# Decay series split between the first products and POOL, first norm inside the fourth x tile, gate banks assigned by hand, and another order at attention's end

## The chip, the cores and the metric

One core of a Trainium2 chip runs the whole program. Its engines work side by side, each through its own list of instructions in order: TensorE does the matmuls (PE in the profile, PEld for its weight loads), VectorE (DVE), ScalarE (ACT) and GpSimd (POOL) do elementwise work, SyncE (SP) and POOL issue DMA transfers. Matmul results lie in eight PSUM banks of 128 x 512 float32. The metric is the device time in microseconds.

## The reference

Two layers on x of shape (1, 512, 1024). Each is a token mixer and then a SwiGLU feed-forward part, with an RMS norm ahead of each part and plain residual adds; a final norm follows. Layer 0 mixes with a gated linear recurrence, layer 1 with stick-breaking attention (16 heads of 64). What bears on the change is the recurrence:

```python
proj = h @ w_in                                  # h = rmsnorm(x)
gate_br, x_br = proj[..., :D_RNN], proj[..., D_RNN:]
gate = gelu(gate_br)
xc = causal_depthwise_conv(x_br, conv_w, conv_b) # width 4
r = sigmoid(blockdiag(xc, w_r) + b_r)            # 4 blocks of 256
i = sigmoid(blockdiag(xc, w_i) + b_i)
log_a = 8.0 * r * log_sigmoid(lam)
a = exp(log_a)
u = sqrt(max(-expm1(2 * log_a), 0)) * (i * xc)
hs = linear_scan(a, u)                           # h_t = a_t h_(t-1) + u_t
return (hs * gate) @ w_out
```

`log_sigmoid(lam)` is a function of 1024 constants; the kernel works it out as a series on a tile of 128 x 8 ("decay").

## The kernel before

**Matmuls.** Every float32 operand is split in a rounded part and a residue (`wh` and `wl` for weights, `uh` and `ul` for activations), and `mm3` makes each product from three matmuls (lines L348 to L350). `mm_tile` does one output tile of 128 x 512 from 8 k-steps of three matmuls. Weights come in chunks of 128 x 1024: SP loads chunk i into one of 4 `raw` buffers, ACT casts it to `wh` (L312), and DVE or POOL subtracts to get `wl` (L313), into 3 buffers each. `wl_on` says which engine does it for chunks 2 to 21; we write wl(i) for this step of chunk i.

**The recurrence (`rglru`).** PE's order is: x tiles 0 and 1 together (`tile_x2`, k by k as x arrives), x tiles 2 to 6, gates(0), x tile 7, gates(1), gate tiles 0 and 1, gates(2), gate tile 2, gates(3), gate tiles 3 to 7, then the output product. x tile m uses chunk m up to 6; chunk 7 belongs to gates(0), chunk 8 to x tile 7. gates(n) has four groups of six matmuls, one bank each.

The norm is applied after the product: `norm_sq` sums the squares of x into `acc` (squares on ACT, adds on DVE, L462), `norm_rs1` forms the row sums with tiny matmuls (L480) and the reciprocal roots on ACT and DVE (`rsqrt`, L467 to L474, which ends with four diagonal blocks `dg`), and `norm_rs2` spreads them over a bank with matmuls (L488) and copies that to `acc` (`rsB`, L489, ACT). `norm_rs1` stands at the middle of x tile 3, `norm_rs2` at the middle of x tile 4.

`evac_x(m)` takes x tile m from its bank once `rsB` is there: times `rsB` (L580, DVE), the convolution (L581 on ACT, three L583 on DVE), and the split into `ah` (L585, ACT) and `al` (L586, DVE), which gates(m // 2) reads. For m of 2 and more the convolution reads the bank itself, so that the bank is free only after the last L583; tiles 0 and 1 are first copied out by L580. evac_x runs for tiles 0 to 2 after x tile 4, then for three more after each further x tile.

`decay` (L561 to L572) is 18 operations on DVE on tiles of 128 x 8, put behind the diagonals by `issue_after`; its results are the scales `ncl`, which gates(0) reads first (L610, tanh on ACT), and `cl`, read by the chain of exponentials (L615). `chain` then does the scan for four tiles (L618 to L624 on DVE). A gate tile leaves its bank by L694 (DVE).

**Banks.** `ps()` hands out the 8 banks in rotation (`bi % 8`). The 2 first x tiles take 0 and 1, tile 2 takes 2, tile 3 takes 3, `norm_rs1` 4, tile 4 5, `norm_rs2` 6, tile 5 7, tile 6 0; gates(0) then takes 1, 2, 3, 4, tile 7 takes 5, gates(1) 6, 7, 0, 1, gate tile 0 takes 2 and gate tile 1 takes 3, gates(2) 4 to 7, gate tile 2 0, gates(3) 1 to 4.

**What sets the order.** In `tile_x2`, in attention's second part and in the feed-forward part the order of the engines' instructions is as written (`manual_schedule`). In the rest of `rglru` a scheduler orders each engine's list by priority (program order; the splits of weights ahead of it) and by when it expects inputs.

**Attention's end.** Heads run in a pipeline: iteration h issues s1(h + 1), chain_a(h + 1), s3(h - 1), s2(h), chain_b(h) and the evacuation `s3_evac(h - 1)` (L1269 on ACT, L1270 on DVE). From h = 13 on one of the two banks for s3 is taken by the output product, so that s3(h) has to wait for s3_evac(h - 1). In iterations 13 and 14 `out_split` also splits a chunk of output weights, with the cast on DVE; in 14 its residue is on DVE too, in 13 on POOL.

Of the kernel before, what the change touches and what calls it, by code (L numbers as in the profile page):

```python
# [10 lines left out]
F32 = mybir.dt.float32  # L11
# [15 lines left out]
RG_C = 8.0  # L27
# [143 lines left out]
class Kern:  # L171
    def __init__(self, ctx, tc, a, out):
        self.ctx, self.tc, self.nc, self.a, self.out = ctx, tc, tc.nc, a, out
        mk = lambda name, bufs, **kw: ctx.enter_context(tc.tile_pool(name=name, bufs=bufs, **kw))
        self.const = mk("const", 1)
        self.wp = mk("wp", 1)
        self.tp = mk("tp", 1)
        self.ar = mk("ar", 1)
        self.free = deque((0, i) for i in range(NS1))
        self.free2 = deque()  # L180
        self.clock = 0
        self.keep2 = 0
        self.slot = {}
        pp = mk("pp", 1, space=bass.MemoryType.PSUM)
        self.bank = [pp.tile([P, S], F32, name=f"bank{i}") for i in range(8)]
        self.bi = 0
        self.tn = 0
        self.later, self.done, self.chain = [], set(), {}
        self.wl_dve = self.wh_dve = False
        self.ring4 = None  # L190
        self.wl_on = {**dict.fromkeys((*range(5, 12), 14, 18, 20, 21), self.nc.gpsimd),
                      **dict.fromkeys((2, 3, 4, 12, 13, 15, 16, 17, 19), self.nc.vector)}

    def ps(self):
        b = self.bank[self.bi % 8]
        self.bi += 1
        return b

# [104 lines left out]
    def split_one(self):  # L303
        i = self.split
        with self.tc.high_priority(self.PRI):
            e = self.chunks[i]
            if isinstance(e, Piece):
                e.sums()
            raw = e.source() if isinstance(e, Piece) else self.raw.pop(i)
            wh, wl = self.split_tiles(i)  # L310
            c = slice(0, raw.shape[-1])
            (self.nc.vector.tensor_copy if self.wh_dve else self.nc.scalar.copy)(wh[:, c], raw)  # L312
            self.wl_engine(i).tensor_tensor(wl[:, c], raw, wh[:, c].bitcast(F32), ALU.subtract)  # L313
            if isinstance(e, Piece):
                e.after()

# [35 lines left out]
    def mm_tile(self, out, xs, mid=None):  # L352
        wh, wl = self.chunk()
        n = len(xs)
        for k in range(n):
            if mid and k == n // 2:
                mid()
            xh, xl = xs[k]
            self.mm3(out, wh[:, ts(k)], wl[:, ts(k)], xh, xl, k == 0, k == n - 1)

# [188 lines left out]
    def rglru(self):  # L549
        nc, tc = self.nc, self.tc  # L550
        with ExitStack() as cx:
# [6 lines left out]
            tc.keep_in_program_order(nc.scalar.preload_act_table_set("natural_log_exp_and_others"))  # L558
            ncl = w

            def decay():  # L561
                nc.vector.tensor_scalar(z, w, 2.0, None, ALU.add)
                nc.vector.reciprocal(z, z)
                nc.vector.tensor_tensor(z, z, w, ALU.mult)
                nc.vector.tensor_tensor(z2, z, z, ALU.mult)
                nc.vector.tensor_scalar(pl, z2, 2.0 / 21, None, ALU.mult)
                for n in (19, 17, 15, 13, 11, 9, 7, 5, 3):
                    nc.vector.scalar_tensor_tensor(pl, pl, 2.0 / n, z2, ALU.add, ALU.mult)
                nc.vector.scalar_tensor_tensor(pl, pl, 2.0, z, ALU.add, ALU.mult)
                nc.vector.scalar_tensor_tensor(cl, lam, 0.0, pl, ALU.min, ALU.subtract)  # L570
                nc.vector.tensor_scalar(cl, cl, RG_C, None, ALU.mult)
                nc.vector.tensor_scalar(ncl, cl, -1.0, 0.0, ALU.mult, ALU.max)  # L572

            def evac_x(m, ps):
                xc[m], ah[m], al[m] = self.new("xc"), self.new("ah", F32R, True), self.new("al", F32R, True)
# [14 lines left out]
            def tile_x(m, mid=None):  # L590
                p = self.ps()
                self.mm_tile(p, self.u, mid)
                return p
# [45 lines left out]
            def tile_x2():  # L639
                p = (self.ps(), self.ps())  # L640
                hl = [self.split_tiles(i) for i in range(2)]
                for k in range(KT):
                    self.norm_in(k, "g_mix0", False)
                    wh, wl = hl[k // 4]
                    if k in self.first:
                        src = self.first[k]
                        c = slice(k % 4 * 2 * P, k % 4 * 2 * P + src.shape[-1])
                        nc.scalar.copy(wh[:, c], src)  # L648
                        nc.vector.tensor_tensor(wl[:, c], src, wh[:, c].bitcast(F32), ALU.subtract)
                    if k == 3:  # L650
                        nc.scalar.activation(w, lam, AF.Abs)
                        nc.scalar.activation(w, w, AF.Exp, scale=-1.0)
                    for i in range(2):
                        c = ts(2 * (k % 4) + i)
                        self.mm3(p[i], wh[:, c], wl[:, c], *self.u[k], k == 0, k == KT - 1)
                nc.gpsimd.memset(self.ones, 1.0)
                nc.gpsimd.memset(self.ident, 0.0)
                nc.gpsimd.affine_select(out=self.ident, in_=self.ident, compare_op=ALU.not_equal, fill=1.0,
                                        base=0, pattern=[[-1, P]], channel_multiplier=1)
                for i in range(2):  # L660
                    self.wq.pop(i)
                self.used = 2
                return p

            pend = []
            for m in range(KT):
                if m == 0:
                    with tc.manual_schedule(engines={mybir.EngineType.Activation, mybir.EngineType.DVE}):
                        pend = list(enumerate(tile_x2()))
                    continue  # L670
                if m == 1:
                    continue
                pend.append((m, tile_x(m, {3: self.norm_rs1, 4: self.norm_rs2}.get(m))))
                if m == 2:
                    with tc.issue_after(self.uhi.ins):
                        for k in range(KT):
                            self.norm_sq(k, nc.vector)
                        nc.scalar.activation(self.st[:, 0:1], self.ones[:, 0:1], AF.Sqrt)
                if m == 3:
                    with tc.issue_after(self.dgi.ins):  # L680
                        decay()
                if m >= 4:
                    for q in pend[:3]:
                        evac_x(*q)
                    pend = pend[3:]
                if m in (6, 7):
                    gates(m - 6)
# [377 lines left out]
    def attention(self):  # L1065
# [5 lines left out]
        with ExitStack() as cx:  # L1071
# [201 lines left out]
            with tc.manual_schedule(engines={E.PE, E.Activation, E.DVE, E.Pool}):  # L1273
# [45 lines left out]
                for h in range(NH + 1):  # L1319
# [40 lines left out]
                        chain_b(h)  # L1360
                    if h == 15:
                        s3(h - 1)
                    if h in (13, 14):
                        out_split()
                    if h >= 1:
                        s3_evac(h - 1)
                    if t < 16 and t % 2 == 0:
                        proj_evac2(t)
                    if 6 <= h < 14 and 2 * nsp + 1 < h:
# [102 lines left out]
```

## Time and profile before

| | |
|---|---|
| median of 3 runs | 1105.23 us (1105.14 to 1107.29) |
| profiled execution | 1105.78 us, span 1104.1 us |
| PE busy | 1088.8 us (99%) |
| DVE, ACT, POOL busy | 901.5 (82%), 709.5 (64%), 363.4 us (33%) |
| mean granted TensorE clock | 0.998 |

The span runs from the first to the last instruction of the program; the profiled execution's own time is 1.7 us longer. Busy times are shares of that span. Matmuls are pipelined, so a busy PE need not be at its peak, and its rows overlap: the distance between two starts tells more than a row's duration.

### The profile page before, as it was taken

The numbers are of one execution on the slowest core, as the hardware profiler recorded it, in microseconds if no ns is written. First come the engines' busy times: TensorE is split into PE (matmuls) and PEld (weight loads), VectorE is DVE, ScalarE is ACT, GpSimd is POOL, SyncE is SP. The second block draws the span as 40 slices with busy tenths as digits, with TensorE's granted clock in tenths as the row PEclk, the third lists the DMA queues.
The fourth block names the chain that finished last, engine by engine and source line by source line (L and its number), as shares of the span: only waits on it lengthen the run. The fifth ranks groups of instructions, "written<-read, shape, count | busy, mean of one in ns | idle before, by whom it ended". The sixth has DMA issues, their size and how long they took to land.

```text
span 1104.1 us, 14724 instructions
## 1 busy us (share of the span) xinstructions
PE 1088.8 (99%) x5255; PEld 907.8 (82%) x5255; DVE 901.5 (82%) x1261; ACT 709.5 (64%) x1084; POOL 363.4 (33%) x251
## 2 busy tenths in 40 slices
PE   9999999999999999999999999999999999999996
PEld 6788888888888888988888888788888888888885
DVE  6978887696978888986378898978679897978897
ACT  6498567565646464635379999967765555546454
POOL 1444242325151514205034445413132424151412
PEclk9999999999999999999999999999999999999999
DMA  8513338887776776343243433225987777775532
GB/s 303 154 59 98 118 111 209 199 191 191 157 200 156 204 155 185 82 152 96 69 122 96 121 90 96 62 94 135 214 175 207 164 186 173 157 199 119 148 69 76
DMA packets 47385, 159.87 MB, mean 145 GB/s; under 512 B 5712, under 2 KB 5968, under 8 KB 47312
## 3 DMA queue, kind: packets, MB, share of 16 engines
q1 hardware_dynamic: 34640, 113.32, 32.0%
q0 software_dynamic: 12384, 45.09, 23.7%
q8 instruction: 41, 0.67, 0.2%
q10 hardware_dynamic: 288, 0.52, 0.1%
q14 instruction: 32, 0.26, 0.1%
HBM read 148.43 MB, written 2.10 MB: 136 GB/s over the span
## 4 chain that ended last, share of the span: by engine, by line
PE 75%; DVE 9%; ACT 4%; issue 3%; DVEq 0%
PE bank L763 17%; PE bank L764 17%; PE bank L765 17%; PE bank L348 6%; PE bank L350 6%; PE bank L349 6%; DVE wl L313 3%; PE bank L1230 2%; DVE y L755 1%; PE bank L770 1%; PE bank L1256 1%; ACT t L1194 1%; ACT t L1193 1%; ACT wh L312 1%; DVE ks L1159 1%
## 5 line engine op out<-in xcount | busy, mean ns | idle before, releaser
L312 ACT CAST wh<-raw 128x1024 fp32r<-128x1024 f32 x134 | 140.2, 1048 | 95.4 <-PE bank L765 36.0
L313 DVE TENSOR_TENSOR wl<-raw,wh 128x1024 fp32r<-128x1024 f32 x112 | 168.3, 1506 | 36.5 <-ACT wh L312 36.4
L763 PE MATMUL bank<-wh,ow 128*128 128x512 f32 (+1 forms) x480 | 179.7, 374 | 0.5 <-DVE b L755 0.5
L765 PE MATMUL bank<-wh,ow 128*128 128x512 f32 (+1 forms) x480 | 178.4, 372 | 0.0
L764 PE MATMUL bank<-wl,ow 128*128 128x512 f32 (+1 forms) x480 | 178.3, 371 | 0.0
L92 POOL DMA_DIRECT2D bu<-w_gu x64 | 56.5, 883 | 275.4 <-DMA bu<-w_gu 147.5
L312 ACT CAST wh<-bu 128x1024 fp32r<-128x1024 f32 x66 | 69.4, 1053 | 65.4 <-PE bank L765 36.1
L313 DVE TENSOR_TENSOR wl<-bu,wh 128x1024 fp32r<-128x1024 f32 x66 | 82.7, 1270 | 30.2 <-ACT wh L312 29.3
L763 PEld LDWEIGHTS bank<-wh,ow 128*128 128x128 f32 x480 | 90.4, 188 | 17.1 <-issue 1.6
L765 PEld LDWEIGHTS bank<-wh,ow 128*128 128x128 f32 x480 | 90.4, 188 | 15.8
L764 PEld LDWEIGHTS bank<-wl,ow 128*128 128x128 f32 x480 | 90.4, 188 | 15.3
L348 PE MATMUL bank<-uh,wh 128*128 128x512 f32 x256 | 102.2, 401 | 0.3 <-ACT wh L648 0.3
L349 PE MATMUL bank<-ul,wh 128*128 128x512 f32 x256 | 99.8, 391 | 0.0
L350 PE MATMUL bank<-uh,wl 128*128 128x512 f32 x256 | 99.6, 391 | 0.0
L755 DVE TENSOR_TENSOR y<-y,bank 128x512 f32<-128x512 f32 x140 | 88.9, 678 | 2.2 <-PE bank L765 2.1
L313 POOL TENSOR_TENSOR wl<-raw,wh 128x1024 fp32r<-128x1024 f32 x24 | 61.1, 2547 | 88.6 <-ACT wh L312 77.5
L763 PE MATMUL bank<-wh,hth 128*128 128x512 f32 (+1 forms) x194 | 75.4, 389 | 0.0
L764 PE MATMUL bank<-wl,hth 128*128 128x512 f32 (+1 forms) x194 | 75.2, 388 | 0.0
L765 PE MATMUL bank<-wh,htl 128*128 128x512 f32 (+1 forms) x194 | 75.1, 387 | 0.0
L313 DVE TENSOR_TENSOR wl<-bv,wh 128x1024 fp32r<-128x1024 f32 x44 | 58.3, 1336 | 13.2 <-ACT wh L312 13.2
L1198 POOL TENSOR_TENSOR spl<-t,sph 128x512 fp32r<-128x512 f32 (+1 forms) x32 | 39.1, 1242 | 82.6 <-DVE sph L1197 80.7
L312 ACT CAST wh<-bv 128x1024 fp32r<-128x1024 f32 x44 | 45.8, 1049 | 18.0 <-PE bank L765 9.0
(276 smaller groups left out, 2776.2 us busy)
## 6 DMA issues: line engine op xcount, KB each, us to landing
bu<-w_gu POOLq DMA_DIRECT2D x64, 512.0 KB, 5.8
raw<-w_gu SPq DMA_DIRECT2D x44, 512.0 KB, 4.0
raw<-w_dn SPq DMA_DIRECT2D x24, 512.0 KB, 5.8
bu<-w_gu SPq DMA_DIRECT2D x22, 512.0 KB, 4.3
bv<-w_gu SPq DMA_DIRECT2D x22, 512.0 KB, 4.2
bv<-w_gu POOLq DMA_DIRECT2D x22, 512.0 KB, 6.4
d<-w_dn SPq DMA_DIRECT2D x20, 512.0 KB, 3.6
raw<-w_qk SPq DMA_DIRECT2D x16, 512.0 KB, 3.6
```

What stands on the lines that cost most here:

```text
L92: kern.soon(lambda: kern.nc.gpsimd.dma_start(t, self.part(n), accum_op=ALU.add))
L312: (self.nc.vector.tensor_copy if self.wh_dve else self.nc.scalar.copy)(wh[:, c], raw)
L313: self.wl_engine(i).tensor_tensor(wl[:, c], raw, wh[:, c].bitcast(F32), ALU.subtract)
L348: mm(out, lhsT=wh, rhs=xh, start=first, stop=False)
L349: mm(out, lhsT=wh, rhs=xl, start=False, stop=False)
L350: mm(out, lhsT=wl, rhs=xh, start=False, stop=last)
L755: add = lambda o, a, b: nc.vector.tensor_tensor(o, a, b, ALU.add)
L763: mm(out, lhsT=xh, rhs=wh, start=first, stop=False, skip_group_check=True)
L764: mm(out, lhsT=xh, rhs=wl, start=False, stop=False, skip_group_check=True)
L765: mm(out, lhsT=xl, rhs=wh, start=False, stop=last, skip_group_check=True)
L1198: nc.gpsimd.tensor_tensor(sl[:, w], sp[:, w], sh[:, w].bitcast(F32), ALU.subtract)
L1230: mm(zt[kt][:, o0:o0 + ZW[j]], lhsT=tri if j == kt else one_n, rhs=s_, start=False, stop=True, skip_group_check=True)
```

## The change

- The decay series is cut in two. Its first five operations (`decay1`) stay on DVE and move ahead of the third k-step of `tile_x2`; their input (Abs and Exp on ACT) moves from the fourth k-step to the second. The other 13 become 24 operations on POOL (`decay2`, a fused DVE operation being two on POOL), issued after wl(7) of x tile 6.
- `norm_rs1` moves from the middle of x tile 3 to after its first k-step, `norm_rs2` from the middle of x tile 4 to after the fifth k-step of x tile 3.
- wl(5) and wl(6) move from POOL to DVE, wl(5) behind the diagonals.
- `ps()` follows a list by hand for its calls 9 to 19: gates(0) gets banks 4, 5, 1, 2, x tile 7 gets 3, gates(1) gets 6, 7, 4, 5, gate tiles 0 and 1 get 1 and 2. By the moved norm x tile 4 lies in bank 6 and `norm_rs2` in 5. gates(3) keeps 1 to 4.
- At attention's end `s3_evac(h - 1)` comes before `out_split`.

```diff
+        self.swap = dict(zip(range(9, 20), (4, 5, 1, 2, 3, 6, 7, 4, 5, 1, 2)))
...
-        self.wl_on = {**dict.fromkeys((*range(5, 12), 14, 18, 20, 21), self.nc.gpsimd),
-                      **dict.fromkeys((2, 3, 4, 12, 13, 15, 16, 17, 19), self.nc.vector)}
+        self.wl_on = {**dict.fromkeys((*range(7, 12), 14, 18, 20, 21), self.nc.gpsimd),
+                      **dict.fromkeys((2, 3, 4, 5, 6, 12, 13, 15, 16, 17, 19), self.nc.vector)}
...
-        b = self.bank[self.bi % 8]
+        b = self.bank[self.swap.pop(self.bi, self.bi % 8)]
...
-            self.wl_engine(i).tensor_tensor(wl[:, c], raw, wh[:, c].bitcast(F32), ALU.subtract)
+            with self.tc.issue_after(self.dgi.ins) if i == 5 else ExitStack():
+                self.wli = self.wl_engine(i).tensor_tensor(wl[:, c], raw, wh[:, c].bitcast(F32), ALU.subtract)
...
-            if mid and k == n // 2:
-                mid()
+            if mid and k in mid:
+                mid[k]()
...
-            def decay():
+            def decay1():
                 nc.vector.tensor_scalar(z, w, 2.0, None, ALU.add)
                 nc.vector.reciprocal(z, z)
                 nc.vector.tensor_tensor(z, z, w, ALU.mult)
                 nc.vector.tensor_tensor(z2, z, z, ALU.mult)
                 nc.vector.tensor_scalar(pl, z2, 2.0 / 21, None, ALU.mult)
-                for n in (19, 17, 15, 13, 11, 9, 7, 5, 3):
-                    nc.vector.scalar_tensor_tensor(pl, pl, 2.0 / n, z2, ALU.add, ALU.mult)
-                nc.vector.scalar_tensor_tensor(pl, pl, 2.0, z, ALU.add, ALU.mult)
-                nc.vector.scalar_tensor_tensor(cl, lam, 0.0, pl, ALU.min, ALU.subtract)
-                nc.vector.tensor_scalar(cl, cl, RG_C, None, ALU.mult)
-                nc.vector.tensor_scalar(ncl, cl, -1.0, 0.0, ALU.mult, ALU.max)
+
+            def decay2():
+                e = nc.gpsimd
+                for c, y in *((2.0 / n, z2) for n in (19, 17, 15, 13, 11, 9, 7, 5, 3)), (2.0, z):
+                    e.tensor_scalar(pl, pl, c, None, ALU.add)
+                    e.tensor_tensor(pl, pl, y, ALU.mult)
+                e.tensor_scalar(cl, lam, 0.0, None, ALU.min)
+                e.tensor_tensor(cl, cl, pl, ALU.subtract)
+                e.tensor_scalar(cl, cl, RG_C, None, ALU.mult)
+                e.tensor_scalar(ncl, cl, -1.0, 0.0, ALU.mult, ALU.max)
...
                 for k in range(KT):
+                    if k == 2:
+                        decay1()
...
-                    if k == 3:
+                    if k == 1:
                         nc.scalar.activation(w, lam, AF.Abs)
                         nc.scalar.activation(w, w, AF.Exp, scale=-1.0)
...
-                pend.append((m, tile_x(m, {3: self.norm_rs1, 4: self.norm_rs2}.get(m))))
+                pend.append((m, tile_x(m, {1: self.norm_rs1, 5: self.norm_rs2} if m == 3 else None)))
...
-                if m == 3:
-                    with tc.issue_after(self.dgi.ins):
-                        decay()
+                if m == 6:
+                    with tc.issue_after(self.wli.ins):
+                        decay2()
...
+                    if h >= 1:
+                        s3_evac(h - 1)
                     if h in (13, 14):
                         out_split()
-                    if h >= 1:
-                        s3_evac(h - 1)
```

## The prediction

> **What bounds the kernel now.** I read the page first, then the list of waits of the matmul engine (PE), then timelines around its longest waits.
>
> ```profile
> span 1104.1 us, 14724 instructions
> ...
> PE 1088.8 (99%) x5255; PEld 907.8 (82%) x5255; DVE 901.5 (82%) x1261; ACT 709.5 (64%) x1084; POOL 363.4 (33%) x251
> ```
>
> PE is busy for 1088.8 of 1104.1 us. The change leaves the matmuls as they are, so all that it can win is idle time of PE, 15.3 us in all, and of that only the waits that it touches. What it does to DVE (82%) or POOL (33%) counts only where PE comes to wait for it. The list of PE's waits (who waits, for whom, us in total, times, longest) has three candidates:
>
> ```profile
> PE bank L348 <- DVE xc L583: 2.1, 1, 2.1
> PE bank L385 <- DVE warm L383: 1.3, 1, 1.3
> PE bank L1256 <- DVE o L1270: 0.9, 2, 0.7
> ...
> PE bank L348 <- DVE gt L694: 0.4, 1, 0.4
> ```
>
> The second is the start. The others stand in PE's timeline as pairs of neighbours (start, duration, idle before):
>
> ```profile
> 48.90 0.39 PE L349 MATMUL bank<-al,wh 128*128 128x512 f32 x1
> 49.13 0.39 PE L350 MATMUL bank<-ah,wl 128*128 128x512 f32 x1
> 51.58 0.47 PE L348 MATMUL bank<-ah,wh 128*128 128x512 f32 x1 [2.06 <-DVE xc L583]
> ...
> 89.85 0.39 PE L350 MATMUL bank<-ah,wl 128*128 128x512 f32 x1
> 90.68 0.50 PE L348 MATMUL bank<-ah,wh 128*128 128x512 f32 x1 [0.44 <-DVE gt L694]
> ...
> 714.14 0.67 PE L1256 MATMUL bank<-awh,vs 128*128 128x512 f32 x2 [0.67 <-DVE o L1270]
> ```
>
> Neighbours normally start 0.23 us apart (48.90 to 49.13). So the first wait costs 2.45 - 0.23 = 2.2 us, the second 0.83 - 0.23 = 0.6, the third its idle time, 0.67.
>
> **Part 1: norm and decay leave DVE's path, and gates(0) gets other banks.** The wait at 51.58 is in the third of the four groups of gates(0). By the rotation this group writes bank 3, which holds x tile 3 until evac_x(3) on DVE is through (its last L583). Why DVE is late, in the timelines of POOL and of DVE:
>
> ```profile
> 26.28 2.71 POOL L313 TENSOR_TENSOR wl<-raw,wh 128x1024 fp32r<-128x1024 f32 x1
> ...
> 30.52 2.38 POOL L313 TENSOR_TENSOR wl<-raw,wh 128x1024 fp32r<-128x1024 f32 x1 [0.68 <-ACT wh L312]
> 39.12 2.85 POOL L313 TENSOR_TENSOR wl<-raw,wh 128x1024 fp32r<-128x1024 f32 x1 [6.22 <-ACT wh L312]
> 45.58 2.40 POOL L313 TENSOR_TENSOR wl<-raw,wh 128x1024 fp32r<-128x1024 f32 x1 [3.61 <-ACT wh L312]
> ```
>
> ```profile
> 20.36 3.87 DVE L462 TENSOR_TENSOR acc<-acc,t 128x512 f32<-128x512 f32 x5
> 27.29 1.74 DVE L470 SCALAR_TENSOR_TENSOR x<-x 128x4 f32<-128x4 f32 x1
> 29.45 0.87 DVE L474 TENSOR_SCALAR t<-x,x 128x128 f32<-128x128 f32 x4
> 30.24 0.17 DVE L562 TENSOR_SCALAR sm<-sm 128x8 f32<-128x8 f32 x1
> 30.68 2.24 DVE L564 TENSOR_TENSOR sm<-sm 128x8 f32<-128x8 f32 x1
> 33.36 1.77 DVE L568 SCALAR_TENSOR_TENSOR sm<-sm 128x8 f32<-128x8 f32 x9
> 35.85 1.28 DVE L580 TENSOR_TENSOR xb<-bank,acc 128x512 f32<-128x512 f32 x2
> ```
>
> (Rows: start, duration, engine, line, operation, tiles, shapes, count, idle before.) The decay series holds DVE from 30.24 to 35.85, 5.6 us; only then does the first evacuation (L580) start. Two tiny operations took ten times the 0.17 of their neighbour: 1.74 and 2.24. Both times POOL was inside a residue operation `wl`, the rows at 26.28 and 30.52. They end at 28.99 and 32.90, DVE's two at 29.03 and 32.92. These two are wl(5) and wl(6), the ones that move to DVE, so both blocks vanish. The Trainium skill says the same ("SBUF — State Buffer", section "Who interferes with whom"): DVE and GpSimd hold a shared port pair exclusively, and a DVE instruction with two SBUF inputs is shut out while a GpSimd instruction reads SBUF. These rows agree, and its other half, that GpSimd waits likewise behind DVE, is a rival below.
>
> When the norm can start:
>
> ```profile
> 23.69 0.39 PE L348 MATMUL bank<-uh,wh 128*128 128x512 f32 x1
> 25.73 0.39 PE L480 MATMUL bank<-x,acc 128*128 128x1 f32 x3
> ...
> 26.54 0.49 PE L348 MATMUL bank<-uh,wh 128*128 128x512 f32 x1
> ...
> 32.13 1.05 PE L488 MATMUL bank<-t,x 128*128 128x128 f32 x8
> ```
>
> Tile 3 starts three matmuls before 23.69, at 23.01. The row sums (L480) come at 25.73, after 12 of its matmuls, and the broadcast (L488) 12 matmuls into tile 4, both exactly where the program puts them, so I take the new places as kept too. Then L480 is due at 23.69, after k = 0, but the sum of squares ends at 20.36 + 3.87 = 24.23 (DVE has nothing less to do before it). PE waits until about 24.3: **a new wait of 0.6 us**. Bounds: 0, if the scheduler lets later matmuls pass, and 0.7 with a semaphore's time on top; I take 0.6, since order was kept before.
>
> ```profile
> 33.22 0.59 ACT L489 COPY acc<-bank 128x512 f32<-128x512 f32 x1 [2.79 <-PE bank L488]
> ```
>
> ```profile
> 16.68 1.23 DVE L313 TENSOR_TENSOR wl<-raw,wh 128x1024 fp32r<-128x1024 f32 x1 [0.25 <-ACT wh L312]
> ```
>
> The chain behind it: from L480's first start to the end of the diagonals (29.45 + 0.87 = 30.32) took 4.6 us; without the block of 1.74 - 0.17 = 1.6 it is 3.0. So they are ready at 27.3. PE meanwhile has eight L480 (0.8 us: 25.73 to 26.54, where tile 3 goes on) and 12 matmuls (2.7 us), and asks for them at 27.8: no wait, 0.5 us of slack. The broadcast and the copy to `acc` on ACT took from 32.13 to 33.81; from 27.8 they end at 29.5. DVE has wl(5) in between, covered by that wait: 1.23 us by DVE's own row of this shape, from 27.3 to 28.5.
>
> So evac_x starts near 29.6 instead of 35.85, 6.2 us sooner; wl(6) takes 1.2 of it back, 5.0 remain. The new banks ask for less besides: gates(0) gets 4, 5 (the norm's, long free), 1 (tile 1, already copied out) and 2 (tile 2). Tile 7 gets bank 3, two groups of six matmuls after the place where the old wait fell. Late by 2.2 before, early by 5: **2.2 us are won**, and the 0.6 above goes off.
>
> decay1 (five tiny DVE operations, at 1.77 / 9 = 0.2 us each, 1.0 us) stands ahead of the third k-step. There DVE idles:
>
> ```profile
> 8.63 0.75 DVE L407 SCALAR_TENSOR_TENSOR ul<-x,x,uh 128x512 fp32r<-128x512 f32 x1 [1.25 <-ACT uh L406]
> ```
>
> ```profile
> 7.87 0.72 ACT L406 ACTIVATE uh<-x,x 128x512 fp32r<-128x512 f32 x1 [1.41 <-DMA x<-xp]
> ```
>
> ```profile
> 7.59 0.54 POOL L1093 TENSOR_SCALAR_AFFINE_SELECT x<-x 128x128 bf16<-128x128 bf16 x2
> ```
>
> 1.25 us hold 1.0; Abs and Exp go into ACT's own hole of 1.41, in which it waits for the DMA of the same x tile. Cost 0; at most 0.3 if POOL's pair of operations at 7.59 (0.54) blocks one of the five (1.0 + 0.54 - 1.25).
>
> decay2 has 24 tiny operations on POOL behind wl(7), the row at 39.12 that ends at 41.97. Nearest row, the reader of decay2's result, and the first matmul of tile 7:
>
> ```profile
> L1198 POOL TENSOR_TENSOR spl<-sp,sph 128x384 fp32r<-128x384 f32 x16 | 19.5, 1219 | 9.1 <-DVE sph L1197 6.9 <-PE bank L1230 2.1
> ```
>
> ```profile
> 54.39 0.39 PE L348 MATMUL bank<-uh,wh 128*128 128x512 f32 x1
> 57.41 0.73 ACT L610 ACTIVATE sv<-r,sm 128x512 f32<-128x512 f32 x1
> ```
>
> Shapes of 384 and 1024 columns take 1.22 (with blocks in it) and 2.40 (45.58): 1.8 ns a column, so 0.5 us for none. The bounds for one are the 0.2 of DVE's tiny ones (33.36) and 1.2; I take 0.3, nearer to the tiny shape. Then decay2 ends at 41.97 + 7.2 = 49.2, and wl(8), queued behind it (2.40), at 51.6. It is needed 0.45 us into tile 7, which now starts at 54.39 - 2.2 + 0.6 = 52.8, so by 53.2. The first reader of the result (L610, 57.41 before) is later still. Cost 0. It turns into a cost at (53.2 - 2.4 - 41.97) / 24 = 0.37 us an operation.
>
> **Part 2: gates(3).** Its wait at 90.68 is for bank 3, its third group, whose holder (gate tile 1) DVE evacuates late:
>
> ```profile
> 63.59 0.78 ACT L581 ACTIVATE xc<-bank,x 128x512 f32<-128x512 f32 x1 [1.71 <-DVE bank L580]
> ...
> 89.97 0.66 DVE L694 TENSOR_TENSOR gt<-bank,acc 128x512 f32<-128x512 f32 x1
> ```
>
> By the new list gate tile 1 lies in bank 2, the second group, so PE asks for it six matmuls (1.4 us) sooner: alone, that makes the wait 0.6 + 1.4 = 2.0. But ACT stood idle for 1.71 us before 63.59, since DVE came to tile 7 late; with DVE 5 us ahead that goes, and everything that ACT and DVE queue behind it up to L694 moves up by at least 1.7 us more than PE does. Taken: the wait vanishes, **0.6 us won**; bounds, 0.6 won and 1.4 lost.
>
> **Part 3: s3_evac before out_split.** At h = 13 DVE has the cast of weights first:
>
> ```profile
> 712.81 0.68 DVE L312 CAST wh<-raw 128x1024 fp32r<-128x1024 f32 x1
> 713.41 0.67 DVE L1270 TENSOR_TENSOR o<-bank,t 64x512 f32<-64x512 f32 x1
> ```
>
> L1270 then starts at 712.81, 0.6 us sooner, and PE's wait of 0.67 shrinks by that: **0.6 us won**. The cast goes back by 0.6, and with it its wl on POOL and the spl (L1198) queued there; PE is asked for nothing of these before s2(15), and the weights are read one iteration on. At h = 14 no PE wait is tied to L1270. Cost 0, at most 0.2.
>
> **Sum:** -2.2 + 0.6 - 0.6 - 0.6 = -2.8 us. The profiled execution took 1105.78 us (its span and 1.7 around it), which gives 1103.0. The median of the three runs, 1105.23, lies 0.55 below that execution, so I predict 1102.5 us. A measurement of this kernel tells about 0.2%, 2.2 us, from no change.
>
> **Rivals.** (A) The banks of gates(3) turn against it, 2.0 instead of 0.6: -2.2 + 0.6 + 1.4 - 0.6 = -0.8, median near 1104.4. For it: L694 stands behind the scans in DVE's order, and the scheduler may keep it there. Against it: ACT's hole of 1.71.
>
> (B) The norm's waits take the place of the old one: PE waits 0.6 for the sums and, if the chain keeps its 4.6 us, another 1.1 at the broadcast (24.3 + 4.6 = 28.9 against 27.8). Sum -2.2 + 1.7 - 0.6 - 0.6 = -1.7, median 1103.5: the change moves the wait and wins too little to be told. For it: 0.5 us of slack only. Against it: POOL has no residue to work on then.
>
> (C) Slower: decay2 crawls on POOL. If every operation first waits out a DVE operation of 0.7 us, one takes about 0.8: 19.2 us, wl(8) ends at 41.97 + 19.2 + 2.4 = 63.6, 10.4 after it is needed; the time is +7.6, near 1113. It loses all gains from 0.49 us an operation on ((53.2 + 2.8 - 2.4 - 41.97) / 24). Against it: most of what DVE does then (L580, L583) reads a bank and one SBUF tile, and wl(7) and wl(8) at 39.12 and 45.58 took 2.85 and 2.40 beside it, hardly blocked. The exclusive lock of the page named above is what would make it so. A further rule of the skill speaks for it: by "GPSIMD Engine Reference", section "2.1 Instruction dispatch", the first call to a freshly loaded kernel on POOL pays about 6 us. No row here shows such a gap; with it decay2 would end near 55, 4.4 us be lost at tile 7, and the sum be +1.6 (an estimate from that page).
>
> **How the numbers follow.** Forecast 0.57, A 0.15, B 0.16, C 0.12. Inside the forecast the size runs from -2.2 (one of the small gains missing) to -3.4 (no wait for the sums), 1101.8 to 1103.1, and the median of few runs adds some 0.5 on each side: its own range is 1101.3 to 1103.6. With A and B, to 1105; C's far end is left out. Faster by over 0.2%: the forecast without its weak edge and a little of B, 0.53; slower: most of C, 0.11; the same: the rest, 0.36.
>
> **What would show it.** L580 starts near 30 instead of 35.85, and PE's waits for L583 and L694 are gone: Part 1 and 2 right. A wait of PE's L480 for `acc` of about 0.5 shows the price. L1270 ahead of L312 near 711, and L1256's longest wait under 0.2: Part 3. Wrong, if PE waits for wl L313 of POOL near 53, or L488 for the diagonals, or L348 for L694 with 1 us or more.

## The result, and the profile after

The changed kernel takes 1102.93 us (median of 8 runs, 1102.49 to 1104.74) beside 1106.72 us for the kernel before (8 runs, 1105.14 to 1108.16): a ratio of 0.9969, 95% interval 0.9958 to 0.9979, some 3.4 us by the ratio (3.8 between the medians). The profiled execution took 1102.71 us; its span fell from 1104.1 to 1101.0. First the head of the page of the changed kernel, then its list of what PE waits for (us in total, times, longest):

```profile
span 1101.0 us, 14735 instructions
...
PE 1087.4 (99%) x5255; PEld 907.8 (82%) x5255; DVE 896.4 (81%) x1250; ACT 710.8 (65%) x1084; POOL 363.5 (33%) x273
```

```profile
PE bank L350 <- ACT wh L656: 1.4, 2, 1.2
PE bank L387 <- DVE warm L385: 1.3, 1, 1.3
...
PE bank L350 <- DVE gt L702: 0.4, 1, 0.4
PE bank L1264 <- DVE o L1278: 0.2, 1, 0.2
```

The wait of 2.1 for x tile 3 is gone from the list. So is the one of 0.67 in attention; the 0.2 for `o` that is left stood beside it before (0.9 in two waits). The one of gates(3) for the gate tile (0.4) is still there. Nothing new stands in the list but a longer wait at the start. Where the time came from shows when the same matmuls are lined up (start, duration): the first of gates(0), the first of tile 7, one ahead of attention, one early in attention, the one in attention whose wait is gone, one near the end. After:

```profile
46.92 0.39 PE L350 MATMUL bank<-ah,wh 128*128 128x512 f32 x1
...
52.36 0.39 PE L350 MATMUL bank<-uh,wh 128*128 128x512 f32 x1
...
466.40 0.39 PE L773 MATMUL bank<-wh,htl 128*128 128x512 f32 x1
...
699.28 0.40 PE L352 MATMUL bank<-oh,wl 128*128 128x512 f32 x1
...
711.39 0.80 PE L1264 MATMUL bank<-awh,vs 128*128 128x512 f32 x3
...
1068.37 0.39 PE L773 MATMUL bank<-wh,htl 128*128 128x512 f32 x1
```

Before (the first of tile 7 stood at 54.39, the one in attention at 714.14):

```profile
46.63 0.39 PE L348 MATMUL bank<-ah,wh 128*128 128x512 f32 x1
...
468.88 0.39 PE L765 MATMUL bank<-wh,htl 128*128 128x512 f32 x1
...
701.77 0.40 PE L350 MATMUL bank<-oh,wl 128*128 128x512 f32 x1
...
1071.46 0.39 PE L765 MATMUL bank<-wh,htl 128*128 128x512 f32 x1
```

The changed kernel is 0.3 late at 46.92, 2.0 ahead at tile 7, 2.5 ahead at 466.40 and still at 699.28, 2.75 ahead at 711.39, and 3.1 ahead at 1068.37. So gates(0) gave 2.3, the stretch from 53 to 466 some 0.4, attention 0.25, the stretch behind it some 0.35 in small pieces, and the start took 0.3. In attention the wait at 711.39 did shrink by 0.6, but PE lost 0.35 just ahead of it, from 709.6 to 710.5, where the lead falls from 2.50 to 2.15. The start is the DMA of an x tile: ACT waited for it until 8.22 here and until 7.87 before.

```profile
8.22 0.72 ACT L408 ACTIVATE uh<-x,x 128x512 fp32r<-128x512 f32 x1 [1.55 <-DMA x<-xp]
```

How the norm runs now, on PE and on DVE:

```profile
23.28 0.39 PE L350 MATMUL bank<-uh,wh 128*128 128x512 f32 x1
...
24.87 0.95 PE L482 MATMUL bank<-x,acc 128*128 128x1 f32 x8
...
27.63 1.05 PE L490 MATMUL bank<-t,x 128*128 128x128 f32 x8
```

```profile
23.87 0.69 DVE L464 TENSOR_TENSOR acc<-acc,t 128x512 f32<-128x512 f32 x1
...
26.43 0.16 DVE L472 SCALAR_TENSOR_TENSOR x<-x 128x4 f32<-128x4 f32 x1
...
29.34 1.29 DVE L586 TENSOR_TENSOR xb<-bank,acc 128x512 f32<-128x512 f32 x2 [0.30 <-ACT acc L491]
```

Tile 3 starts at 23.28, but the row sums (L482) come at 24.87, after seven of its matmuls and not after three. The last sum of squares ends at 23.87 + 0.69 = 24.56, so PE waits for nothing. The tiny operation that took 1.74 before takes 0.16, and the first evacuation (L586) starts at 29.34 instead of 35.85.

The series on POOL: its first operation, a plain one, its last, and the residues behind it:

```profile
39.99 0.57 POOL L573 TENSOR_SCALAR sm<-sm 128x8 f32<-128x8 f32 x1
...
40.85 0.20 POOL L574 TENSOR_TENSOR sm<-sm 128x8 f32<-128x8 f32 x1
...
48.15 0.26 POOL L578 TENSOR_SCALAR sm<-sm 128x8 f32<-128x8 f32 x1
48.37 5.22 POOL L315 TENSOR_TENSOR wl<-raw,wh 128x1024 fp32r<-128x1024 f32 x2
```

24 operations in 48.41 - 39.99 = 8.4 us: 0.35 each on average, of which the typical 0.20 to 0.24 is work and the rest the step to the next; three of them took 0.57, 0.69 and 0.67. wl(8) begins at 48.37.

The wait that stayed, at gates(3): on PE, then DVE's chain that leads to it, after and (second fence, its first row alone) before:

```profile
86.14 0.39 PE L352 MATMUL bank<-ah,wl 128*128 128x512 f32 x1
86.93 0.50 PE L350 MATMUL bank<-ah,wh 128*128 128x512 f32 x1 [0.41 <-DVE gt L702]
...
68.97 1.30 DVE L624 SCALAR_TENSOR_TENSOR sv<-t,sv 128x512 f32<-128x512 f32 x2 [2.53 <-ACT t L623]
...
86.22 0.66 DVE L702 TENSOR_TENSOR gt<-bank,acc 128x512 f32<-128x512 f32 x1
```

```profile
72.72 1.30 DVE L618 SCALAR_TENSOR_TENSOR sv<-t,sv 128x512 f32<-128x512 f32 x2 [2.53 <-ACT t L617]
```

From the chain's first row to the gate tile's evacuation it is 17.25 us in both (68.97 to 86.22, 72.72 to 89.97): a rigid block, moved up by 3.75 as a whole. And the attention's two operations, in their new order:

```profile
710.66 0.67 DVE L1278 TENSOR_TENSOR o<-bank,t 64x512 f32<-64x512 f32 x1
711.26 0.67 DVE L313 CAST wh<-raw 128x1024 fp32r<-128x1024 f32 x1
```

### The profile page after: what moved, and what is told of

Its sections match the earlier page's. It is cut to its first block, busy times and chain, and to the rows that moved or that the text cites. A ratio compares the mean times of both kernels' runs of the same rounds, so it can differ in the third digit from the quotient of the medians.

```text
span 1101.0 us, 14735 instructions
## 1 busy us (share of the span) xinstructions
PE 1087.4 (99%) x5255; PEld 907.8 (82%) x5255; DVE 896.4 (81%) x1250; ACT 710.8 (65%) x1084; POOL 363.5 (33%) x273
## 4 chain that ended last, share of the span: by engine, by line
PE 75%; DVE 9%; ACT 4%; issue 3%; DVEq 0%
PE bank L771 17%; PE bank L772 17%; PE bank L773 17%; PE bank L350 6%; PE bank L352 6%; PE bank L351 6%; DVE wl L315 3%; PE bank L1238 2%; DVE y L763 1%; PE bank L778 1%; PE bank L1264 1%; ACT t L1202 1%; ACT t L1201 1%; ACT wh L313 1%; DVE ks L1167 1%
## 5 line engine op out<-in xcount | busy, mean ns | idle before, releaser
L315 DVE TENSOR_TENSOR wl<-raw,wh 128x1024 fp32r<-128x1024 f32 x114 | 171.6, 1507 | 39.9 <-ACT wh L313 39.5
L315 POOL TENSOR_TENSOR wl<-raw,wh 128x1024 fp32r<-128x1024 f32 x22 | 55.8, 2540 | 80.1 <-ACT wh L313 68.4
L350 PEld LDWEIGHTS bank<-uh,wh 128*128 128x128 f32 x256 | 48.0, 188 | 11.5 <-ACT wh L656 2.5
```

The costliest lines, as they stand in the source:

```text
L315: self.wli = self.wl_engine(i).tensor_tensor(wl[:, c], raw, wh[:, c].bitcast(F32), ALU.subtract)
L350: mm(out, lhsT=wh, rhs=xh, start=first, stop=False)
```

## The experiments

The theory (D in the expectations): the gain is VectorE's time. PE pays where VectorE is late, and any part counts only by how much sooner VectorE gets on. The rivals put the gain elsewhere: in the banks by hand (K), in the series leaving VectorE, in the port that VectorE shares with POOL; or they see a price in POOL's load (C of the prediction). All comparisons are with the kernel before, on the same chip.

**1. The banks, each way.** The changed kernel with the plain rotation:

```diff
-        self.swap = dict(zip(range(9, 20), (4, 5, 1, 2, 3, 6, 7, 4, 5, 1, 2)))
+        self.swap = {}
```

> The changed kernel with the plain rotation of banks in place of the list by hand: gates(0) gets 1, 2, 3, 4, x tile 7 gets 5, gates(1) 6, 7, 0, 1, gate tiles 0 and 1 get 2 and 3. Theory D (DVE starts the evacuations 6.5 us sooner, and this alone ends PE's wait in gates(0)): tile 3 leaves bank 3 by about 46, the third group asks for it at 49.7, so no wait comes back; gate tile 1 is asked for in the third group of gates(3) again, 1.4 us later than now, so the 0.6 us left there go too: span about 1100.4. Theory K (the banks by hand end the wait, DVE's earlier start is not needed): the wait for L589 comes back in the third group of gates(0), up to 2.2 us: span about 1103.

And the kernel before with such a list and nothing else:

```diff
+        self.swap = dict(zip(range(9, 20), (4, 6, 1, 2, 3, 5, 7, 4, 6, 1, 2)))
...
-        b = self.bank[self.bi % 8]
+        b = self.bank[self.swap.pop(self.bi, self.bi % 8)]
```

> The kernel before with banks by hand alone, fitted to its own place of the norm: gates(0) gets 4, 6, 1, 2, x tile 7 gets 3, gates(1) 5, 7, 4, 6, gate tiles 0 and 1 get 1 and 2. Decay, norm and splits stay as they were. Theory K: PE's wait of 2.1 us goes and nothing comes for it; gates(3) asks 1.4 us sooner for gate tile 1: span 1104.1 - 2.2 + 1.4 = 1103.3 at the most, 1101.9 at the least. Theory D: DVE is as late as before, so the wait moves on, to gates(1), which asks for banks 5 and 7 (tiles 4 and 5) 2 us sooner, and to gates(3): span 1103.5 to 1104.5.

Without the list: 1102.06 us (9 runs), ratio 0.9966 (0.9956 to 0.9976), span 1100.4, no wait at gates(0), and none at gates(3) either. With the list alone: 1108.45 us (10 runs), ratio 1.0022 (1.0013 to 1.0032), slower than before. Its list of waits and PE's rows say why:

```profile
PE bank L351 <- DVE wl L314: 2.4, 1, 2.4
```

```profile
79.37 0.39 PE L350 MATMUL bank<-ul,wh 128*128 128x512 f32 x1
82.12 0.51 PE L351 MATMUL bank<-uh,wl 128*128 128x512 f32 x1 [2.36 <-DVE wl L314]
```

At gates(0) PE no longer waits, so it arrives sooner at a gate tile whose residue VectorE makes as late as ever: the wait of 2.1 has become one of 2.4, 30 us on. K falls. The banks only choose where PE meets the late engine. (The clock fell behind this wait, see the last section. The profiled execution, 1106.6 us, was the fastest of the ten, so what the others lost besides is not shown; the median lies above what either theory expected.)

**2. The attention's order alone**, in the kernel before:

```diff
+                    if h >= 1:
+                        s3_evac(h - 1)
                     if h in (13, 14):
                         out_split()
-                    if h >= 1:
-                        s3_evac(h - 1)
```

> The kernel before with only the order at attention's end changed: s3_evac ahead of out_split. If this part gives 0.6 us on its own, PE's longest wait for o (0.67) goes, L1270 starts at once behind L1211 and the span is 1103.5. If the weights' cast that now comes later is asked for at once, another wait of PE takes its place and the span stays at 1104.1.

1105.51 us (10 runs), ratio 0.9994 (0.9985 to 1.0003): by its time not to be told from no change. In the trace the wait of 0.67 for `o` is gone and the one of 0.2 is left, as in the changed kernel; here nothing is lost ahead of it. The span (1104.2) does not show it, since this execution lost 1.6 us elsewhere. The stretches just behind the wait at gates(0) (us, busy time of PE and its matmuls, of PEld, DVE, ACT, POOL, then PEclk, DMA share, GB/s), here and in the kernel before:

```profile
51.50:55.20 3.70, 3.66 (x9) 2.89 (x10) 3.41 (x6) 3.67 (x6) 0.88 (x1) 0.55 0.46 132
```

```profile
51.50:55.20 3.70, 3.62 (x16) 3.06 (x17) 3.40 (x6) 3.65 (x5) 0.91 (x1) 1.00 0.45 132
```

Both had the same wait, of 2.45 us from matmul to matmul. After it one ran 16 matmuls at the full clock, the other 9 at a granted clock of 0.55. The last section comes back to this.

**3. The list carried on** to gates(3), so that the gate tile's bank is asked for last:

```diff
-        self.swap = dict(zip(range(9, 20), (4, 5, 1, 2, 3, 6, 7, 4, 5, 1, 2)))
+        self.swap = dict(zip((*range(9, 20), *range(25, 29)), (4, 5, 1, 2, 3, 6, 7, 4, 5, 1, 2, 1, 3, 4, 2)))
```

> The changed kernel with the list of banks carried on to gates(3): 1, 3, 4, 2 in place of 1, 2, 3, 4, so that gate tile 1 (bank 2) is asked for by the fourth group and not by the second, 2.7 us later. If PE's wait for L702 is about the time of asking alone, it goes (L702 ends at 86.9, the fourth group asks at 89.1) and the span is 0.6 us shorter, 1100.4. If the scans on DVE set the pace of this stretch whatever is asked for, the wait moves to gate tile 2 or to the next group and the span stays at 1101.0.

1101.8 us (5 runs, 1101.38 to 1102.0), ratio 0.996 (0.9947 to 0.9972), span 1099.7; the wait for L702 is gone. It is the fastest version of all, though part of its span is a start without the DMA's delay, and by the ratios alone it can't be told from the changed kernel.

**4. The series' second half on VectorE**, as 13 fused operations behind the diagonals, instead of 24 on POOL:

```diff
-                e = nc.gpsimd
-                for c, y in ...
+                for n in (19, 17, 15, 13, 11, 9, 7, 5, 3):
+                    nc.vector.scalar_tensor_tensor(pl, pl, 2.0 / n, z2, ALU.add, ALU.mult)
...
-                if m == 6:
-                    with tc.issue_after(self.wli.ins):
+                if m == 3:
+                    with tc.issue_after(self.dgi.ins):
```

> The changed kernel with the second part of the decay series back on DVE, as 13 fused operations of 0.2 us right behind the diagonals (so the evacuations start 2.6 us later, near 32 instead of 29.3). Theory D with slack (in the changed kernel DVE is some 3 us or more ahead of what PE asks, so POOL is not needed for the series): no new wait of PE, span 1101.0. Theory P (the move to POOL is what pays): part of the old wait in gates(0), or a wait at gate tile 2, comes back, 1 to 2 us: span 1102 to 1103.

1103.27 us (10 runs), ratio 0.9975 (0.9966 to 0.9985), span 1101.6, 0.6 above the changed kernel's. There is still no wait at gates(0). The one at gates(3) grew:

```profile
PE bank L350 <- DVE gt L700: 1.3, 1, 1.3
```

VectorE is 0.7 later there (L700 at 86.90, L702 at 86.22), and PE waits 0.9 longer. So the move to POOL is worth something, but at gates(3), through the list of banks, and not at gates(0).

**5. The residues wl(5) and wl(6) back on POOL:**

```diff
-        self.wl_on = {**dict.fromkeys((*range(7, 12), 14, 18, 20, 21), self.nc.gpsimd),
+        self.wl_on = {**dict.fromkeys((*range(5, 12), 14, 18, 20, 21), self.nc.gpsimd),
...
-            with self.tc.issue_after(self.dgi.ins) if i == 5 else ExitStack():
+            with ExitStack():
```

> The changed kernel with wl(5) and wl(6) back on POOL and wl(5) not held behind the diagonals. On POOL wl(5) stands behind the first DMA issue, which ends at 26.8, so it runs from about 26.5 to 29.0, while DVE is at the reciprocal roots (26.2 to 27.0) and PE asks for the diagonals at 27.6. Theory of the shared port: one tiny operation on DVE waits until 29.0, the diagonals end at 30.2, PE waits about 2 us at L490 (and if its clock falls after such a wait, 1.4 us more): span 1103 to 1104.4. Theory that DVE's tiny operations are slow by themselves: no wait, span 1101.0.

1110.02 us (8 runs), ratio 1.003 (1.0019 to 1.0042), span 1106.5: 5.5 more than the changed kernel's span, and above all that was expected. PE's waits, DVE's operation and POOL's:

```profile
PE bank L490 <- DVE t L476: 2.5, 1, 2.5
PE bank L350 <- DVE gt L702: 1.8, 1, 1.8
```

```profile
25.80 3.08 DVE L472 SCALAR_TENSOR_TENSOR x<-x 128x4 f32<-128x4 f32 x1
...
26.20 2.65 POOL L315 TENSOR_TENSOR wl<-raw,wh 128x1024 fp32r<-128x1024 f32 x1
```

A tiny operation issued at 25.80 ends at 28.88, with POOL's residue (28.85): 0.16 of work and 2.9 of standing still. The Trainium skill's page "SBUF — State Buffer" (section "Who interferes with whom") states this lock for a VectorE instruction with two SBUF inputs; the rows agree in where both end. (POOL's row begins 0.4 us after VectorE's, which the lock by itself does not explain.) PE asks for the diagonals with no slack now, so the block, hidden before in a norm that was late anyhow, lands on PE. The expectation had this wait and the slowed clock behind it (PEclk 0.56); what it missed is the second wait, at gates(3), where 0.4 became 1.8.

**6. POOL's load doubled:** 24 more tiny operations, on a tile that nobody reads, between the others.

```diff
+                for c, y in *((2.0 / n, z2) for n in (19, 17, 15, 13, 11, 9, 7, 5, 3, 19, 17)), (2.0, z):
+                    e.tensor_scalar(jk, pl, c, None, ALU.add)
+                    e.tensor_tensor(jk, jk, y, ALU.mult)
```

> The changed kernel with 24 more tiny operations on POOL behind the series, into a tile that nobody reads. In the changed kernel the 24 take 8.4 us (40.0 to 48.4, 0.35 each) and wl(8) follows them. Theory of my third rival (the series on POOL has little room): wl(8) ends 8.4 us later, near 59.3, tile 7 asks for it at 52.8, PE waits about 6.5 us and its clock may fall after it (1.4 us): span 1107.5 to 1109. Theory that POOL is off the path here: span 1101.0.

1111.46 us (4 runs), ratio 1.005 (1.0035 to 1.0065), span 1110.2. Now PE waits for POOL's wl(8), and the clock falls behind that wait:

```profile
PE bank L352 <- POOL wl L315: 5.9, 1, 5.9
```

```profile
59.60:64.60 5.00, 5.00 (x13) 3.84 (x13) 0.00 (x0) 0.00 (x0) 5.00 (x3) 0.50 0.72 209
```

Rival C had the right place where a late POOL is paid for, but not its crawl: an operation took 0.35 us, not 0.8. With 24 operations it costs nothing, with 48 the kernel is slower than before. The expectation allowed 1.4 us for the clock; it stayed at half for 6.8 us (57.74 to 64.57), which cost about 3.

**7. The norm back at its old places**, all else as changed:

```diff
-                pend.append((m, tile_x(m, {1: self.norm_rs1, 5: self.norm_rs2} if m == 3 else None)))
+                pend.append((m, tile_x(m, {3: {4: self.norm_rs1}, 4: {4: self.norm_rs2}}.get(m))))
```

(and banks 5 and 6 exchanged in the list, since the norm then takes them in another order).

> The changed kernel with the norm's two steps at their old places (middle of x tiles 3 and 4) and the banks by hand fitted to that (gates(0) 4, 6, 1, 2, tile 7 3, gates(1) 5, 7, 4, 6). The broadcast comes 4.5 us later, so the evacuations start near 34 instead of 29.3, still 2 us before the 35.85 of the kernel before. If DVE's start is what counts, and its lead is about 5 us, PE just gets by or waits up to 1 us: span 1101 to 1102. If the norm's place does not matter: 1101.0, and DVE idle between the diagonals and the broadcast.

Expected was a span of 1101 to 1102; measured were 1106.13 us (10 runs), ratio 0.9997 (0.9988 to 1.0007), and a span of 1105.9 in the profiled execution, the slowest of the ten: **all of the gain is gone**, or nearly so. This miss points at the norm's place. The series is off VectorE here, the residues do not block it, and yet the first evacuation comes at 33.92:

```profile
33.92 1.29 DVE L586 TENSOR_TENSOR xb<-bank,acc 128x512 f32<-128x512 f32 x2 [2.15 <-ACT acc L491]
```

VectorE idles 2.15 us for the norm's broadcast. With the norm late no evacuation can start sooner. The 4.6 us (33.92 against 29.34) shrink to 2.2 at gates(3) (L702 at 88.43 against 86.22), and PE pays in two waits and, behind the first of the two listed, with a slowed clock:

```profile
PE bank L350 <- DVE gt L702: 1.8, 1, 1.8
...
PE bank L352 <- DVE wl L315: 0.7, 1, 0.7
```

This run does not show that the other parts are worth nothing without the norm's move, since it keeps the list of banks, which by itself made the kernel before slower (run 1). By its rows VectorE is 1.93 us ahead of the kernel before (33.92 against 35.85), where PE's wait at gates(0) was 2.2. So with the plain rotation some 0.3 of that wait would be left, and gates(3) would ask 1.4 later: an estimate. That version, and the residues moved alone, were not run.

**8. The norm early, the series as before.** That miss asked for the converse, in two forms. The changed kernel with the series back whole on VectorE:

```diff
-                    if k == 2:
-                        decay1()
...
-                if m == 6:
-                    with tc.issue_after(self.wli.ins):
-                        decay2()
+                if m == 3:
+                    with tc.issue_after(self.dgi.ins):
+                        decay()
```

> The changed kernel with the decay series put back whole on VectorE (18 tiny operations behind the norm's diagonals, as before); norm, residues, banks and attention as changed. Theory D (a late VectorE decides, and PE pays at gates(3), where the list of banks asks for gate tile 1 early): 18 x 0.20 = 3.6 us of VectorE work, of which some 1.3 us lie in its hole before the first evacuation; the run with 13 operations came 0.7 us later at L702, so here L702 comes 1.0 to 2.0 us later than in the changed kernel, the matmul that waits for it starts 1.8 to 2.8 us after its neighbour (0.80 there), and the span is 1102.1 to 1103.0. Theory H (beside D: a hole of more than about 2 us can cost PE its full clock for some 3 us): then 1.4 us more, up to 1104.4, in part of the runs, so a median of 1104 to 1105.5 and a spread of over 1.5 us. Rival N (the norm's earlier place carries the gain alone, the split of the series is worth nothing): a span of 1101.0 and a median of 1102.9.

And the kernel before with the norm's new places and the two residues on VectorE, nothing else:

```diff
-            if mid and k == n // 2:
-                mid()
+            if mid and k in mid:
+                mid[k]()
...
-                pend.append((m, tile_x(m, {3: self.norm_rs1, 4: self.norm_rs2}.get(m))))
+                pend.append((m, tile_x(m, {1: self.norm_rs1, 5: self.norm_rs2} if m == 3 else None)))
...
+            with self.tc.issue_after(self.dgi.ins) if i == 5 else ExitStack():
```

> The kernel before with the norm's row sums and broadcast at their new places inside the fourth x tile and the first two residues on VectorE, and nothing else: series whole on VectorE, banks by plain rotation, attention's order as before. Theory D: the norm gives VectorE 4 to 5 us, the series keeps 1 to 2 of the 5.6 that it held; gates(0) asks for its bank some 2.5 us before VectorE's old time, so its wait goes (at most 0.5 us is left), as does that at gates(3), since the rotation asks for gate tile 1 later; the 0.67 us in attention stay. Span 1101.5 to 1102.3, median about 1103.3. Rival S (the split of the series is needed for gates(0)): a wait of 1 to 2 us stays there, span 1102.5 to 1104. Rival N: as much as the changed kernel, 1101.0.

The norm with the two residues: 1103.24 us (7 runs), ratio 0.9973 (0.9963 to 0.9984), by the ratios 3.0 us of the changed kernel's 3.4, and within the intervals not to be told from it. (Its profiled execution, 1105.5 us, was the slowest of the seven: matmul by matmul it stays within 0.3 us of the changed kernel up to 205 us and then loses 2.5 between 214 and 230, which the changed kernel's profile lacks; its median speaks for it, and its first 200 us.) No wait is left at gates(0), and 0.4 at gates(3). Rival S falls. Why the series costs PE so little now, in VectorE's timeline of this kernel:

```profile
29.09 0.69 DVE L582 TENSOR_TENSOR xb<-bank,acc 128x512 f32<-128x512 f32 x1
29.70 0.16 DVE L566 TENSOR_TENSOR sm<-sm 128x8 f32<-128x8 f32 x1
29.77 0.68 DVE L582 TENSOR_TENSOR xb<-bank,acc 128x512 f32<-128x512 f32 x1
...
37.39 2.37 DVE L570 SCALAR_TENSOR_TENSOR sm<-sm 128x8 f32<-128x8 f32 x1
...
41.83 0.69 DVE L582 TENSOR_TENSOR bank<-bank,acc 128x512 f32<-128x512 f32 x1
```

Before, the 18 operations ran one behind another, each 0.20 us after the last, and one was blocked for 2.24. Here the evacuations can already start, the scheduler sets the tiny ones between them, and each delays its neighbour by 0.07 (29.70 to 29.77), all but one: at 37.39 one took 2.37, while POOL was at a residue (37.04 to 39.74). So the series is not free for VectorE. The evacuation of x tile 3 starts at 41.83, in the changed kernel at 38.21, 3.6 sooner. It costs PE nothing at gates(0) because the norm's move left more slack there than that.

In the changed kernel with its list of banks the same series costs 1.2 us by the medians, 1.5 by the ratios (1104.14 us, 11 runs, ratio 0.9983, 0.9974 to 0.9992). The wait is at gates(3), 2.18 from matmul to matmul (0.80 in the changed kernel):

```profile
86.05 0.39 PE L352 MATMUL bank<-ah,wl 128*128 128x512 f32 x1
88.22 0.50 PE L350 MATMUL bank<-ah,wh 128*128 128x512 f32 x1 [1.79 <-DVE gt L696]
```

It fits the expectation under D (1.8 to 2.8 there, a median of 1104 to 1105.5 with the clock in part of the runs, a spread of over 1.5: 1102.77 to 1106.33).

## Why the prediction was right, step by step

The forecast of 1102.5 us (median 1102.93), its mechanism at gates(0) and the sum (1103.0 for the profiled execution, 1102.71 measured) held. That the sum came so close is partly luck: two terms of 0.6, one a price and one a gain, were both wrong and cancelled, and what attention fell short by (0.35) came in from places that the sum does not have. The median, too, was counted from three runs before (1105.23) that lay 1.5 below the median of the eight: the gain forecast was 2.8, the measured one 3.4 by the ratio.

- **gates(0), -2.2:** right. The evacuations start at 29.34 (said 29.6), tile 7 comes 2.3 sooner relative to gates(0). But the reason given put the series first ("holds DVE from 30.24 to 35.85, 5.6 us"). Run 8 turns it round: with the series left whole on VectorE, the norm's move and the two residues win 3.0 of 3.4. Run 7 wins nothing without the norm's move, but under a list of banks that costs time by itself there.
- **The new wait of 0.6 at the row sums:** wrong, and with it rival B. The step that failed is "exactly where the program puts them, so I take the new places as kept too": the row sums stand four matmuls further back than the program has them, at 24.87, and the sum of squares was through at 24.56. The bound of 0 was the right end.
- **decay1, 0:** right; VectorE waited 0.76 for ACT behind it.
- **decay2, 0:** right in its outcome. An operation took 0.35 us and not 0.3, near the limit of 0.37 worked out there; but POOL came to the series 2 us sooner than said (39.99, not 41.97). wl(8) is through near 51.0 (48.37 and half of the 5.22), 1.8 us before tile 7 needs it (52.36 + 0.45). That margin agrees with run 6: there wl(8) ended at 58.75, 7.8 later; less 1.8 leaves 6.0, and the wait was 5.9. The page's 6 us for a first call on POOL ("GPSIMD Engine Reference", "2.1 Instruction dispatch" in the Trainium skill) do not appear: the first operation took 0.57, beside 0.24 for the others of its kind.
- **gates(3), -0.6:** wrong; the measured term is 0 (0.83 before, 0.80 after). The step that failed is "the wait vanishes". VectorE's block did move 1.4 more than PE (3.75 against 2.36 at the first matmul of gates(3)), 0.3 short of the "at least 1.7" that was said; and the list asks 1.4 sooner, which rival A had turned into a wait of 2.0. The two shifts cancel, and the wait stays as it was. Runs 1 and 3, where the bank is asked for later, have no such wait: that 0.6 is what the list costs.
- **Attention, -0.6:** right for the wait it names (the rows at 710.66 and 711.26, and run 2 alone), but in the changed kernel only 0.25 arrived, since PE lost 0.35 just ahead of it (709.6 to 710.5). What caused that loss stays open; run 2 lacks it.
- **Left out:** some 0.3 lost at the start, which comes and goes with a DMA, and what a wait can do to the clock (below). The kernel before has a hole of 2.45 us at gates(0); executions in which the clock then falls would lie some 1.6 us higher, as the one of run 2 did. That could be why the ratio (3.4) exceeds the difference of the two spans (3.1); it was not tested by itself.

## What to carry to other kernels

A late engine is paid for where the matmul engine meets it. Here new banks alone only moved the long wait to another place, and an earlier start of the late engine removed it; so look for the chain that everything behind it waits for (here a norm of 4.6 us) before counting the busy time that it holds. A long series of tiny operations is dear where it stands alone between two dependent steps (0.20 us each here) and cheaper where other work can lie between (0.07 us each, but for one that was blocked), and its price counts only beyond the slack that is there. When a list is written by hand, follow it to its end: this one cured a wait that was gone anyway, and kept another alive behind it.

## What the runs showed of the hardware

The matmul clock falls behind shorter holes than expected, and not each time. What decides is how much of one 3.41 us window is idle. The granted clock in the traces changes only on such a grid: in the run of the attention's order alone it is 1.00 up to 51.87, 0.50 to 55.28 and 1.00 again, and its next fall, at the end (1099.76), lies 307 times 3.413 us behind the first. So the last fall of a trace gives the grid of a run in which the clock does not fall before. In the table: holes from matmul to matmul, the mean granted clock in the stretch behind them, and the idle share of PE's rows in the window that holds most of the hole.

| kernel | hole, us | clock behind it | idle share of the window |
|---|---|---|---|
| before | 2.45 | 1.00 | 44% (47.62 to 51.03) |
| attention's order alone | 2.45 | 0.55 | 60% (48.46 to 51.87) |
| series whole on VectorE | 2.18 | 1.00 | 46% (86.67 to 90.08) |
| norm at its old places | 2.18 | 0.54 | 52% (87.13 to 90.54) |
| banks alone | 2.75 | 0.55 | 69% (79.07 to 82.48) |
| wl(5), wl(6) on POOL, first | 2.88 | 0.56 | 73% (26.45 to 29.87) |
| wl(5), wl(6) on POOL, second | 2.14 | 1.00 | 40% (91.31 to 94.72) |
| POOL's load doubled | 6.31 | 0.50 | 100% (54.33 to 57.74) |

The rows of the two holes of 2.18, from the stretch where the clock differs:

```profile
90.00:93.30 3.30, 3.30 (x16) 2.74 (x15) 1.04 (x1) 2.58 (x4) 1.50 (x1) 1.00 0.75 202
```

```profile
90.90:94.20 3.30, 3.30 (x10) 2.58 (x9) 1.06 (x1) 1.38 (x2) 1.38 (x1) 0.54 0.64 201
```

In the same 3.3 us one ran 16 matmuls, the other 10. So a wait of 2 us costs its own 2 us in one execution and some 1.5 more in another, by where it falls on the grid: the five windows at full clock with 52% and more of idle time were each followed by one at half clock, and none with 46% or less was (the start and the end of the program left out). The limit between the two is not known closer. With POOL's load doubled the clock stayed at half for a second window; the first of the two was 31% idle. No hole of up to 1.65 us was followed by such a stretch in the profiles here, the first 8 us left out. The Trainium skill's page "TensorE: Matmul & The Clock Gate" (section "Why this matters for your kernels") asks for no holes above about 3 us; these runs put the limit lower, at about 2 us where the hole lies in one window. The same page (section "What's actually happening") states that the activity is judged in windows of 3.4 us that run freely. The grid in these traces agrees, with 3.413 us, and the table shows how the same hole counts in one execution and not in another.
